# Moving the matmul operands of a fused encoder layer to other places modulo 256 bytes

## The chip, the cores and the metric

The kernel runs on one core of one Trainium2 chip. The metric is the device time of one execution in microseconds; the number that counts is the median of several executions. A profile of one execution gives what each engine did; a matmul runs on the TensorE (PE in the profile), which loads a stationary operand (PEld, the weight load) and streams a moving operand past it. Both are read from the on-chip memory SBUF, 128 partitions of 224 KiB each; the sums go to the eight PSUM banks. VectorE is DVE, ScalarE is ACT, GpSimd is POOL, SyncE is SP.

## The reference

One layer on 512 tokens with a model width of 1024, all float32. Shifts, scales and gates (`sh`, `sc`, `g`) come from a conditioning vector.

```python
h = modulate(rmsnorm(x, norm_ffn1), sh1, sc1)
x = x + 0.5 * g1 * swiglu(h, w_ffn1_in, w_ffn1_out)          # width 2816

h = modulate(rmsnorm(x, norm_mix), sh2, sc2)
qa, ka, va, qb, kb, vb, ga, gb = split(h @ w_in)
ya = window_gqa_sink(rope(norm(qa)), rope(norm(ka)), va, sink) @ w_branch_a
ob = diff_attention(rope(norm(qb)), rope(norm(kb)), vb, lam)
yb = (rmsnorm(ob, subln) * 0.8) @ w_branch_b
x = x + g2 * ((sigmoid(ga) * ya + sigmoid(gb) * yb) @ w_out)

h = modulate(rmsnorm(x, norm_ffn2), sh3, sc3)
x = x + 0.5 * g3 * swiglu(h, w_ffn2_in, w_ffn2_out)
```

## The kernel before

**Arithmetic.** Every float32 operand of a product is split into a high part (rounded to the PE's one-pass float32 type) and the low rest. A product is three matmuls into one bank: high by high, high by low, low by high (`mm3`, L172 to L175; the same three in `two`, L456 to L458). Weights are split by `split_from` (L189): ACT writes the high part, DVE the low one. In the mixer `load_main` (L1115) has ACT write a copy and its negative, and a DMA of POOL's queue adds the weights to the latter.

**Stages in order of time.** The first part of the first feed-forward runs at 512 columns (`first_products`, L703, and `mm3`). From about 82 us it runs in 256 columns: a `Unit` (L460) computes a pair of hidden blocks with seven products of half size instead of eight, named `a11`, `a12`, `s1`, `s2`, `s3`, `s4`, `a22`, each of 4 x 2 x 3 = 24 matmuls. Four times a stretch of 512 columns stands between them: `Out1` (L891), the second matrix of the feed-forward, in four chunks (`CHUNKS`). The last four blocks of the last chunk run by halves, 256 columns (`by_halves`, L906). Three gates follow, also by halves (`first_gates`, L1147), and then the mixer: projections at 512 columns with the weights moving and `h` stationary (`project`), the same in 256 columns (`project_pairs`, L1198), gates at 512 columns (`gates`, L1227), and between them, interleaved by a planner, the scores and products of two attentions (`diff_out` L1403, `window_out` L1640, 256 columns). Then come the branches (`branch`, L1665), the output product (L1729, its last two blocks by halves) and the second feed-forward. That one starts with a plain unit (`Plain`, L1820: four weight sets, no sums) interleaved with `units[1]`, called `lead`, and goes on in units of seven products to the end; the second matrix is also done in units there. The order of the matmuls is the order in which the program lists them.

**Operands of a unit.** The moving operands are the halves of `h` and four sums and differences of them (`SUMS`, L581): `n1`, `n2`, `t3`, `t4`. All lie in the twelve buffers called `b8`, but `n1`, which lies in two of the six buffers called `u4` (L605; `u` in the profile). In the second feed-forward's second matrix a few of the activations lie in `u4` too (L1789). Weights lie in `high` and `low`, two tiles of five places each, which `high_low` (L196) hands out in turn; `aside` shifts a place by so many elements of 4 bytes. Two weight sets of `lead` lie in `b8` (`apart`, L1843), and the weights of the three first gates in `u4` (`spare`, L1144).

**Where the tiles lie.** The allocator puts the groups of equal tiles one behind the other in the order of their first use, each rounded up to 32 bytes per partition. Adding up the sizes gives each start; modulo 256 bytes they are: `x`, `high`, `low`, `ka` and `b8` at 64, `u4` at 160, `raw` and `f2` at 192. All buffers of one group have the same place modulo 256, since their sizes are multiples of 256, and so have all slices that a 256- or 512-column matmul takes from them. In `high` and `low` place i begins at i x 1024 elements plus 64 for each of the first two, both multiples of 256 bytes, plus `aside`. So a weight set lies at 64 with `aside` 0 or `FAR` (64 elements are 256 bytes), at 128 with `ASIDE` (16), at 160 with `TURN` (24). This document calls the stationary operand's place minus that of the moving one, modulo 256 bytes, the **distance** of a matmul.

```python
        i = i * 1024 + min(i, 2) * GAP + aside          # L203, in high_low
        return tuple(t[:, i : i + n] for t in parts)
```

The distances before are then, by stage:

| matmuls | columns | moving | stationary | distance |
|---|---|---|---|---|
| first part, `Out1`, `project`, most gates and branches | 512 | 64 | 64 | 0 |
| units, moving operand in `b8` or `ka` | 256 | 64 | 128 | 64 |
| units, moving operand in `u4` (`n1` and some activations) | 256 | 160 | 128 | 224 |
| last blocks of `Out1`, of a branch, of the output product; `a11`, `a21` of `Plain` | 256 | 64 | 128 or 160 | 64 or 96 |
| three first gates | 256 | 64 | 160 | 96 |
| `project_pairs` | 256 | 128 | 64 | 192 |
| `diff_out`, `window_out`, `s1` of `lead` | 256 | 160 | 64 | 160 |
| `a12` of `lead` | 256 | 64 | 64 | 0 |
| the gate with number `EARLY_A` | 512 | 64 | 128 | 64 |

Of the kernel before, what the change touches and what calls it, by code (L numbers as in the profile page):

```python
# [12 lines left out]
F32R = mybir.dt.float32r  # L13
I32 = mybir.dt.int32
# [4 lines left out]
P = 128  # L19
D = 1024  # L20
T = 512
NC = D // P
NT = T // P
# [9 lines left out]
SH1, SC1, G1, SH2, SC2, G2, SH3, SC3, G3 = range(9)  # L33
# [63 lines left out]

RAW, HILO, F2 = 5, 5, 8

ASIDE, TURN, GAP = 16, 24, 64  # L100

FAR = 64


BRANCH_ASIDES = (ASIDE, TURN, ASIDE, ASIDE), (ASIDE,) * 4
MIX_ASIDES = 0, 0, 0, 0, 0, 0, ASIDE, ASIDE

CHUNKS = (range(0, 6), range(6, 12), range(12, 16), range(16, 22))
PLAIN, LAST_1 = 3, 4
# [24 lines left out]
def layer(ctx: ExitStack, tc: tile.TileContext, a: dict):  # L134
# [13 lines left out]
    def xt():  # L148
        return sbuf("x", [P, T], F32, 8)
# [16 lines left out]
    def keep(shape, nm, dt=F32):  # L166
        return sb.tile(shape, dt, name=nm, tag=nm, bufs=1)
# [28 lines left out]
    def high_low(n=1024, aside=0, holder=None):  # L196
        while turn[0] % HILO in holders:
            turn[0] += 1
        i = turn[0] % HILO
        turn[0] += 1  # L200
        if holder:
            holders[i] = holder
        i = i * 1024 + min(i, 2) * GAP + aside  # L203
        return tuple(t[:, i : i + n] for t in parts)

    def let_go(holder):
# [24 lines left out]
    sub8, lam_s, nlam = (keep([P, n], nm) for nm, n in (("sub8", 1), ("lam_s", 2), ("nlam", 1)))  # L231
    rqa, ccol = keep([P, NT, 8], "rqa"), small(NC)
    x = [xt() for _ in range(NC)]
    parts, modv = [], []
    for nm, n in (("high", 6), ("low", 0)):
        parts.append(keep([P, HILO * 1024 + 2 * GAP + ASIDE], nm, F32R))
        modv += [keep([P, NC], f"mod{v}") for v in range(n)]

    def load_by(t, src, n):
# [9 lines left out]
        return w  # L249


    begin, begins, norms = keep([P, 6 * NC], "begin"), {}, {SC1: NORM1, SC2: NORM2, SC3: NORM3}

    def mod_begin(v):
        if v in (SH1, SH2, SH3):
# [204 lines left out]
    class Unit:  # L460
# [12 lines left out]
        MAKE = {"s1": 5, "a11": 3, "a12": 2, "s2": 4, "s4": 2, "s3": 2, "a22": 3}  # L473
        asked, length = ("s1", "a11", "a12", "a22"), 1.0

        in_order = turned = by_columns = ()
        spare, roomy, apart, more = ("s1",), (), (), {"s1": ("s2", "a11"), "s2": ("s4", "a12"), "a11": ("s3", "a21")}

        def place(self, q):
# [14 lines left out]
        def prepare(self, q):  # L494

            if q in self.ready:
                return
            self.ask(q)
            n = self.depth * 2 * P
            if q in self.apart:  # L500
                both = b8().rearrange("p a b -> p (a b)")
                hi, lo = both[:, 0:n], both[:, 1024 : 1024 + n]
            else:
                hi, lo = high_low(n, TURN if q in self.turned else ASIDE, (self, q))
            t = self.at[q]
            with tc.issue_after(copied[0]) if q in self.in_order and copied else nullcontext():
                split_from(hi, lo, t)
            self.ready[q] = hi, lo
            if q in self.more:
                s, src = self.more[q]  # L510
                G.dma_start(t, self.srcs[src], accum_op=ALU.add)
                self.at[s] = t
# [103 lines left out]
    cact = [sbuf("ka", [P, D], F32, 1)]  # L616
    hh, hl = new_h()
    modv += [keep([P, NC], f"mod{v}") for v in range(len(modv), 9)]
    nc.scalar.dma_start(ccol, a["c"])
    tc.keep_in_program_order(nc.scalar.dma_start(par, a["par"]))  # L620
    for c in range(NC):
# [2 lines left out]
    with tc.manual_schedule(engines=BOUND | {mybir.EngineType.SP, mybir.EngineType.Pool}):  # L624
# [24 lines left out]
        def first_loads(k):  # L649
            n = 1 if k else 2  # L650
            scale = mod_load(SC1, k, n=n)
            if k == 0:
                kept.append(keep([P, NT], "pos", I32))
            shift = mod_load(SH1, k, n=n) if k == 0 else None
            raw = sbuf("raw", [P, 1024], F32, RAW)
            load_by(raw, a["w1s"][k], n)
            w1[k] = [scale, shift or mod_load(SH1, k), raw]
# [227 lines left out]
    def in_unit1(p):  # L885
        srcs = {q: a["w1u"][p - PLAIN, i] for i, q in enumerate(("a11", "a12", "a21", "a22"))}
        u = Unit(srcs, 4, h1_operand, in_post1, p % 2)
        u.p, u.in_order = p, ('s2', 's4')
        return u

    class Out1:  # L891
# [17 lines left out]
        def prepare(self, m):  # L909
            if m not in self.ready:  # L910
                self.ask(m)
                aside = FAR if not self.by_halves(m) else TURN if m < NC - LAST_1 + 2 else ASIDE
                if self.final and m == 0:
                    while turn[0] % HILO != 1:
                        turn[0] += 1
                t = self.ready[m] = high_low(self.depth * P, aside, (self, m))
                with tc.issue_after(copied[0]):
                    split_from(*t, self.at[m])
# [279 lines left out]
    def project_pairs(srcs, then):  # L1198

        n = 2 * P  # L1200
        out = [bank("acc") for _ in range(2)]
        for u, src in enumerate(srcs):
            wh, wl = load_main(src, ASIDE)
            for t in range(NT):
                ht = slice(t * P, (t + 1) * P)
                po = out[t // 2][:, t % 2 * n : (t % 2 + 1) * n]
                for i in range(4):
                    k = 4 * u + i
                    w = slice(i * n, (i + 1) * n)
                    first, last = k == 0 and t % 2 == 0, k == NC - 1 and t % 2 == 1  # L1210
                    PE.matmul(po, hh[k][:, ht], wh[:, w], start=first, stop=False, skip_group_check=True)
                    PE.matmul(po, hh[k][:, ht], wl[:, w], start=False, stop=False, skip_group_check=True)
                    PE.matmul(po, hl[k][:, ht], wh[:, w], start=False, stop=last, skip_group_check=True)
                    yield MM3 / 2
        then(out)
# [11 lines left out]
    def gates(more=lambda: True):  # L1227
        while gate_next[0] < 16 and more():
            j = gate_next[0]
            gate_next[0] += 1  # L1230

            wh, wl = load_main(a["w_gate"][j], ASIDE * (j == EARLY_A))
            out = bank("acc")
            for k in range(NC):
                o = k * P
                mm3(out, wh[:, o : o + P], wl[:, o : o + P], hh[k], hl[k], k == 0, k == NC - 1)
                yield MM3
            gate_end(j, out)
# [423 lines left out]
            turns["w"] = (b, g * nk + kc + 1)  # L1662


    def branch(w, j0, o_h, o_l, then, load, r=FULL[0], asides=(0, 0, 0, 0)):  # L1665
        for u in range(4):
            with tc.issue_after(banded_last[0]):
                wh, wl = load(w[u], aside=asides[u])
            for i in range(2):
                j = 2 * u + i  # L1670
                g = f2()[:, r]
                nc.sync.dma_start(g, gate_scr[j0 + j][:, r])
                y = bank("acc")[:, r]
                for k in range(4):
                    o = k * 256 + i * P
                    mm3(y, wh[:, o : o + P], wl[:, o : o + P], o_h[:, k, r], o_l[:, k, r], k == 0, k == 3)
                    yield MM3 * (r.stop - r.start) / T
                then(j, g, y, r)

    def main():  # L1680
        yield from beside(project(vb_w, T, values_b), LATER)
        yield from beside(project(a["w_kb"], T, keys_b), LATER)
        yield from beside(project(a["w_qb"], T, queries_b), LATER)
        yield from beside(gates(lambda: gate_next[0] < EARLY_A), 1)
        while later or asked:
            column(later)
        tables_a()
        yield from project_pairs([a["w_kva"][u] for u in range(2)], keys_a)
        for g in range(2):
            yield from project_pairs([a["w_qa"][2 * g + u] for u in range(2)], lambda ps, g=g: queries_a(ps, g))  # L1690
        yield from gates(lambda: done["b"] < NT)
        line.drain(lambda: done["b"] == NT)
        start_a()
        yield from gates()
        ma = [b8(F32) for _ in range(2)]

        def then_a(j, g, y, r):
            V.scalar_tensor_tensor(ma[j // 4][:, j % 4, r], g, 1.0, y, ALU.add, ALU.mult)
            line.helped(0.6)

        yield from branch(a["w_yb"], 8, ob_h, ob_l, then_a, load_main)
        mix.extend(new_h())
        mh, ml = mix

        def then_b(j, g, y, r):
            V.scalar_tensor_tensor(g, g, 1.0, y, ALU.add, ALU.mult)
            m = ma[j // 4][:, j % 4, r]
            V.tensor_tensor(m, m, g, ALU.add)
            split_from(mh[j][:, r], ml[j][:, r], m)
            line.helped(1.0)  # L1710

        for i, r in enumerate(HALVES):
            line.drain(lambda: done["a"] >= 2 * i + 2)
            yield from branch(a["w_ya"], 0, *wa["o"], then_b, load_halves, r, BRANCH_ASIDES[i])

    mix = []
    line.run(main())
# [120 lines left out]
            V.scalar_tensor_tensor(g, g, -1.0, self.bank[1, t], ALU.mult, ALU.mult)  # L1838

    plain = units[0] = Plain(units[0].srcs, 4, h_operand, None, 0)  # L1840
    plain.turned = ("a11", "a21")
    lead = units[1]
    lead.spare, lead.roomy, lead.apart = ("s1", "a11", "a12"), ("a22",), ("s1", "a12")  # L1843
    for u in units[1:]:
# [254 lines left out]
```

## Time and profile before

| | us |
|---|---|
| median of 3 executions | 1039.54 |
| lowest and highest of them | 1039.32, 1040.16 |
| the profiled execution | 1039.97 |
| its span, first to last instruction | 1038.2 |
| outside its span | 1.77 |

The profiled execution is 0.43 us over the median. Its granted TensorE clock is 1.00 throughout. A row of a group in the profile reads: line, engine, operation, output and inputs by the program's names with buffer numbers left out, shape, count, then busy us, mean ns of one record, and the idle time before. A matmul's record is longer than the distance between two starts, since matmuls are pipelined; the page says that their ends are modelled. Stretches of the trace are named by their time from the span's start.

### The profile page before, as it was taken

The numbers are of one execution on the slowest core, as the hardware profiler recorded it, in microseconds if no ns is written. First come the engines' busy times: TensorE is split into PE (matmuls) and PEld (weight loads), VectorE is DVE, ScalarE is ACT, GpSimd is POOL, SyncE is SP. The second block draws the span as 40 slices with busy tenths as digits, with TensorE's granted clock in tenths as the row PEclk, the third lists the DMA queues.
The fourth block names the chain that finished last, engine by engine and source line by source line (L and its number), as shares of the span: only waits on it lengthen the run. The fifth ranks groups of instructions, "written<-read, shape, count | busy, mean of one in ns | idle before, by whom it ended". The sixth has DMA issues, their size and how long they took to land.

```text
span 1038.2 us, 18851 instructions
## 1 busy us (share of the span) xinstructions
PE 1030.8 (99%) x7346; PEld 951.1 (92%) x7346; DVE 786.9 (76%) x1456; ACT 583.9 (56%) x1014; POOL 162.5 (16%) x190
## 2 busy tenths in 40 slices
PE   9999999999999999999999999999999999999998
PEld 7789899899999998899888888989999999999998
DVE  7786667567796679859782598976899777877877
ACT  6665335244364343667785856525867546654553
POOL 1101110110110100543333101001112112112210
PEclk9999999999999999999999999999999999999999
DMA  9977787966884459796737944974498998989974
GB/s 360 356 238 203 233 231 209 257 166 205 253 203 133 152 192 410 236 288 139 186 69 190 254 134 151 364 252 104 94 237 191 243 229 207 224 223 214 211 156 112
DMA packets 70377, 220.92 MB, mean 213 GB/s; under 512 B 8464, under 2 KB 13200, under 8 KB 70288
## 3 DMA queue, kind: packets, MB, share of 16 engines
q1 hardware_dynamic: 47808, 146.52, 39.0%
q0 software_dynamic: 19344, 68.70, 35.9%
q10 hardware_dynamic: 3136, 4.51, 1.2%
q8 instruction: 57, 0.93, 0.3%
q14 instruction: 32, 0.26, 0.1%
HBM read 209.46 MB, written 10.23 MB: 212 GB/s over the span
## 4 chain that ended last, share of the span: by engine, by line
PE 94%; DMA 2%; DVE 2%; ACT 2%; issue 0%; SPq 0%; DVEq 0%; ACTq 0%
PE acc L457 7%; PE acc L458 7%; PE acc L456 7%; PE sc L457 6%; PE sc L458 6%; PE sc L456 6%; PE sc L173 5%; PE sc L174 5%; PE sc L175 5%; PE acc L173 5%; PE acc L175 5%; PE acc L174 5%; PE tp L1270 2%; DMA raw<-w1s 2%; PE acc L1192 2%; PE acc L1194 2%
## 5 line engine op out<-in xcount | busy, mean ns | idle before, releaser
L189 ACT CAST high<-raw 128x1024 fp32r<-128x1024 f32 (+2 forms) x176 | 158.2, 913 | 152.9 <-PE sc L174 40.4
L189 DVE TENSOR_TENSOR low<-raw,high 128x1024 fp32r<-128x1024 f32 (+2 forms) x176 | 183.2, 1050 | 42.1 <-ACT high L189 40.8
L456 PE MATMUL acc<-b,high 128*128 128x256 f32 x508 | 140.9, 277 | 0.0
L457 PE MATMUL acc<-b,high 128*128 128x256 f32 x508 | 140.7, 277 | 0.1
L458 PE MATMUL acc<-b,low 128*128 128x256 f32 x508 | 140.6, 277 | 0.0
L457 PE MATMUL sc<-b,high 128*128 128x256 f32 x500 | 138.2, 276 | 0.0
L456 PE MATMUL sc<-b,high 128*128 128x256 f32 x500 | 138.1, 276 | 0.0
L458 PE MATMUL sc<-b,low 128*128 128x256 f32 x500 | 138.1, 276 | 0.0
L189 ACT CAST high<-u 128x1024 fp32r<-128x1024 f32 (+1 forms) x73 | 75.5, 1035 | 50.5 <-PE sc L174 20.2
L189 DVE TENSOR_TENSOR low<-u,high 128x1024 fp32r<-128x1024 f32 (+1 forms) x73 | 87.6, 1200 | 20.4 <-ACT high L189 18.8
L173 PE MATMUL sc<-b,high 128*128 128x512 f32 (+1 forms) x272 | 97.5, 358 | 0.0
L174 PE MATMUL sc<-b,high 128*128 128x512 f32 (+1 forms) x272 | 97.2, 357 | 0.0
L175 PE MATMUL sc<-b,low 128*128 128x512 f32 (+1 forms) x272 | 97.1, 357 | 0.0
L457 PEld LDWEIGHTS acc<-b,high 128*128 128x128 f32 x508 | 95.5, 188 | 0.4 <-DVE b L1883 0.3
L456 PEld LDWEIGHTS acc<-b,high 128*128 128x128 f32 x508 | 95.5, 188 | 0.3 <-ACT f L534 0.2
L458 PEld LDWEIGHTS acc<-b,low 128*128 128x128 f32 x508 | 95.4, 188 | 0.0
L458 PEld LDWEIGHTS sc<-b,low 128*128 128x128 f32 x500 | 93.9, 188 | 0.0
L456 PEld LDWEIGHTS sc<-b,high 128*128 128x128 f32 x500 | 93.9, 188 | 0.0
L457 PEld LDWEIGHTS sc<-b,high 128*128 128x128 f32 x500 | 93.9, 188 | 0.0
L173 PE MATMUL acc<-b,high 128*128 128x512 f32 (+1 forms) x240 | 89.0, 371 | 0.0
L175 PE MATMUL acc<-b,low 128*128 128x512 f32 (+1 forms) x240 | 86.7, 361 | 0.0
L174 PE MATMUL acc<-b,high 128*128 128x512 f32 (+1 forms) x240 | 86.5, 361 | 0.0
(397 smaller groups left out, 2715.9 us busy)
## 6 DMA issues: line engine op xcount, KB each, us to landing
u<-w_mod SPq DMA_DIRECT2D x38, 512.0 KB, 8.3
b<-w_mod SPq DMA_DIRECT2D x32, 512.0 KB, 5.5
raw<-w2i SPq DMA_DIRECT2D x31, 512.0 KB, 5.4
u<-w2i POOLq DMA_DIRECT2D x31, 512.0 KB, 6.7
raw<-w1u SPq DMA_DIRECT2D x24, 512.0 KB, 7.1
u<-w1u POOLq DMA_DIRECT2D x24, 512.0 KB, 7.1
raw<-w1o SPq DMA_DIRECT2D x24, 384.0 KB, 4.4
raw<-w_gate SPq DMA_DIRECT2D x16, 512.0 KB, 5.2
```

The lines of the kernel that those rows point to most:

```text
L173: PE.matmul(out, wh, xh, start=first, stop=False)
L174: PE.matmul(out, wh, xl, start=False, stop=False)
L175: PE.matmul(out, wl, xh, start=False, stop=last)
L189: last = S.copy(hi, src), V.tensor_tensor(lo, src, f(hi), ALU.subtract)
L456: PE.matmul(out, wh[:, s], xh, start=first and j == 0, stop=False, skip_group_check=True)
L457: PE.matmul(out, wh[:, s], xl, start=False, stop=False, skip_group_check=True)
L458: PE.matmul(out, wl[:, s], xh, start=False, stop=last and j == 1, skip_group_check=True)
L1192: PE.matmul(out[t][:, 0:n], hh[k][:, ht], wh[:, o : o + n], start=k == 0, stop=False)
L1194: PE.matmul(out[t][:, 0:n], hl[k][:, ht], wh[:, o : o + n], start=False, stop=k == NC - 1)
L1270: PE.transpose(tp[:, j * P : (j + 1) * P], src, ident)
```

## The change

Nothing is computed otherwise, no operation is added or left out, and no order written in the program is changed. What changes are starts in SBUF. A place in `high` and `low` is now 1088 elements long (4352 bytes, a multiple of 256) and has a lead of 16 elements, two pads of 192 and 160 bytes and longer `begin` and `pos` tiles shift what lies behind, and the ring of descriptors for DMAs of POOL's queue is halved to make room.

```diff
-ASIDE, TURN, GAP = 16, 24, 64
+ASIDE, FIRST, GAP = 16, -8, 64
...
-BRANCH_ASIDES = (ASIDE, TURN, ASIDE, ASIDE), (ASIDE,) * 4
-MIX_ASIDES = 0, 0, 0, 0, 0, 0, ASIDE, ASIDE
+MIX_ASIDES = 0, 0, 0, 0, 0, 0, FIRST, ASIDE
...
-        i = i * 1024 + min(i, 2) * GAP + aside
+        i = i * (1024 + GAP) + ASIDE + aside
...
     x = [xt() for _ in range(NC)]
+    keep([P, 48], "pad1")
...
-        parts.append(keep([P, HILO * 1024 + 2 * GAP + ASIDE], nm, F32R))
+        parts.append(keep([P, HILO * (1024 + GAP) + ASIDE], nm, F32R))
...
-    begin, begins, norms = keep([P, 6 * NC], "begin"), ...
+    begin, begins, norms = keep([P, 6 * NC + ASIDE], "begin"), ...
...
-                hi, lo = high_low(n, TURN if q in self.turned else ASIDE, (self, q))
+                hi, lo = high_low(n, self.asides.get(q, ASIDE), (self, q))
...
     modv += [keep([P, NC], f"mod{v}") for v in range(len(modv), 9)]
+    keep([P, 40], "pad2")
...
-                kept.append(keep([P, NT], "pos", I32))
+                kept.append(keep([P, 2 * NC], "pos", I32)[:, 0:NT])
...
         u.p, u.in_order = p, ('s2', 's4')
+        if p == PLAIN:
+            u.asides = {"s1": FIRST}
+        elif 2 * p in [c.start for c in CHUNKS[1:]] or p == PLAIN + 1:
+            u.asides = {"s2": FIRST}
...
-                aside = FAR if not self.by_halves(m) else TURN if m < NC - LAST_1 + 2 else ASIDE
+                aside = (FIRST if m == NC - LAST_1 else ASIDE) if self.by_halves(m) else FAR
...
-            wh, wl = load_main(src, ASIDE)
+            wh, wl = load_main(src, -ASIDE)
...
-            wh, wl = load_main(a["w_gate"][j], ASIDE * (j == EARLY_A))
+            wh, wl = load_main(a["w_gate"][j])
...
-            yield from branch(a["w_ya"], 0, *wa["o"], then_b, load_halves, r, BRANCH_ASIDES[i])
+            yield from branch(a["w_ya"], 0, *wa["o"], then_b, load_halves, r, (ASIDE if i else FIRST,) + (ASIDE,) * 3)
...
-    plain.turned = ("a11", "a21")
+    plain.asides = {"a11": FIRST}
...
-    nc = bacc.Bacc("TRN2", target_bir_lowering=False, num_devices=1, dynamic_dma_scratch_size=4096)
+    nc = bacc.Bacc("TRN2", target_bir_lowering=False, num_devices=1, dynamic_dma_scratch_size=2048)
```

Adding up the sizes again: the first pad puts `high` at 0 modulo 256 instead of 64; `high` is 21824 bytes long, and with the six small tiles behind it `low` is at 0 too. With the new lead of 64 bytes a weight set lies at 64 with `aside` 0 or `FAR`, at 128 with `ASIDE`, at 32 with `FIRST`, at 0 with `-ASIDE`. `b8` and `ka` stay at 64, `u4` moves from 160 to 64, `raw` and `f2` from 192 to 128. So the distances become:

| matmuls | distance before | after |
|---|---|---|
| 512 columns | 0 (one gate: 64) | 0 |
| units, moving operand in `b8` or `ka` | 64 | 64 |
| units, moving operand in `u4` | 224 | 64 |
| the first weight set behind a stretch of 512 columns (`s1` of the first unit; `s2` of units 4, 6, 8; block 4 of the last `Out1`; set 0 of the first half branch; block 6 of the output product) | 224, 64, 96, 64, 64 | 224 |
| other blocks by halves there | 64 or 96 | 64 |
| `a11` of `Plain`, `a21` of `Plain` | 96, 96 | 224, 64 |
| three first gates | 96 | 0 |
| `project_pairs` | 192 | 64 |
| `diff_out`, `window_out`, `s1` of `lead` | 160 | 0 |
| `a12` of `lead` | 0 | 0 |

More of the change, by code (lines that the diff above doesn't have):

```diff
@@ L249, in mod_load @@
         return w
-    begin, begins, norms = keep([P, 6 * NC], "begin"), {}, {SC1: NORM1, SC2: NORM2, SC3: NORM3}
+    begin, begins, norms = keep([P, 6 * NC + ASIDE], "begin"), {}, {SC1: NORM1, SC2: NORM2, SC3: NORM3}
     def mod_begin(v):
@@ L474, in layer @@
         asked, length = ("s1", "a11", "a12", "a22"), 1.0
-        in_order = turned = by_columns = ()
+        in_order, by_columns, asides = (), (), {}
         spare, roomy, apart, more = ("s1",), (), (), {"s1": ("s2", "a11"), "s2": ("s4", "a12"), "a11": ("s3", "a21")}
@@ L1662, in window_out, with branch @@
             turns["w"] = (b, g * nk + kc + 1)
-    def branch(w, j0, o_h, o_l, then, load, r=FULL[0], asides=(0, 0, 0, 0)):
+    def branch(w, j0, o_h, o_l, then, load, r=FULL[0], asides=(0,) * 4):
         for u in range(4):
```

## The prediction

> **What bounds the kernel.** I read the page first: the busy shares and the chain of waits.
>
> ```profile
> span 1038.2 us, 18851 instructions
> PE 1030.8 (99%) x7346; PEld 951.1 (92%) x7346; DVE 786.9 (76%) x1456; ACT 583.9 (56%) x1014; POOL 162.5 (16%) x190
> PE 94%; DMA 2%; DVE 2%; ACT 2%; issue 0%; SPq 0%; DVEq 0%; ACTq 0%
> ```
>
> PE is 94% of the chain that ends last, and no other engine is above 76%. So the pace of the matmuls themselves sets the time, and I asked for the groups of PE with shapes kept apart.
>
> ```profile
> L174 PE MATMUL sc<-b,high 128*128 128x512 f32 x192 | 74.8, 390 | 0.0
> L456 PE MATMUL acc<-b,high 128*128 128x256 f32 x508 | 140.9, 277 | 0.0
> L457 PE MATMUL acc<-u,high 128*128 128x256 f32 x80 | 22.3, 279 | 0.0
> L457 PE MATMUL sc<-u,high 128*128 128x256 f32 x72 | 20.1, 280 | 0.0
> L1212 PE MATMUL acc<-low,b 128*128 128x256 f32 x96 | 26.9, 280 | 0.0
> L175 PE MATMUL op<-u,b 128*128 128x256 f32 x72 | 20.3, 282 | 0.0
> L456 PE MATMUL acc<-b,b 128*128 128x256 f32 x8 | 2.3, 283 | 0.0
> ```
>
> The last column is idle time: there is none. Yet a matmul of 256 columns takes 277 to 283 ns, and what differs between the rows is where the operands lie: distance 64 in the second row, 224 in the third and fourth, 192, 160 and 0 in the last three. To turn a record into a pace, I took three neighbouring stretches, of 24, 24 and 144 matmuls by the timeline, from the view of stretches, and the records within the first and the last.
>
> ```profile
> 142.57:145.40 2.83, 2.83 (x26) 1.00 0.91 262
> 145.40:148.20 2.80, 2.80 (x26) 1.00 1.02 399
> 148.20:164.50 16.30, 16.30 (x146) 1.00 1.00 263
> L457 PE MATMUL acc<-b,high 128*128 128x256 f32 x8 | 2.2, 281 | 0.0
> L457 PE MATMUL acc<-b,high 128*128 128x256 f32 x24 | 6.6, 276 | 0.0
> ```
>
> The first stretch needs 2.83 / 24 = 117.9 ns per matmul with a record of 281, the third 16.30 / 144 = 113.2 with 276. So a nanosecond of record is about one of pace, and the records can be used as prices. But both stretches have distance 64, on the same operand groups. The distance alone does not decide: at 64 there is a **light** pace (276) and a **heavy** one (281). Heavy is what follows a stretch of 512 columns; the 24 matmuls at 224 in between (`n1`) turn it light. Other stretches, each a row of a window of its own, in order of time:
>
> ```profile
> L457 PE MATMUL acc<-b,high 128*128 128x256 f32 x21 | 5.9, 281 | 0.0
> ...
> L174 PE MATMUL sc<-b,high 128*128 128x256 f32 x11 | 3.1, 280 | 0.0
> ...
> L174 PE MATMUL sc<-b,high 128*128 128x256 f32 x12 | 3.4, 281 | 0.0
> ...
> L174 PE MATMUL acc<-b,u 128*128 128x256 f32 x36 | 10.1, 280 | 0.0
> ...
> L174 PE MATMUL acc<-b,high 128*128 128x512 f32 x7 | 2.8, 395 | 0.0
> ...
> L174 PE MATMUL acc<-b,high 128*128 128x256 f32 x8 | 2.2, 280 | 0.0
> ...
> L174 PE MATMUL sc<-b,high 128*128 128x256 f32 x18 | 5.1, 281 | 0.0
> ```
>
> They are: behind a wait of PE at 315 us (64, heavy); the last blocks of the first feed-forward at 340 us (distance 96) and 344 us (64, heavy); the three first gates at 364 us (96); the one gate of 512 columns at distance 64, at 502 us; a branch set at 649 us (96); the output product at 701 us (64, heavy, right behind 512 columns).
>
> **The change, part by part.** Nothing issued changes, so each part is a count of matmuls times a difference of records. (a) Moving operands in `u4`: the lines L456 to L458 have 3 x (80 + 72) = 456 of them at 279 to 280. 24 stay at 224 (the first set at 82 us); 432 go to distance 64. If they run light, 432 x 3.5 ns = -1.5 us. (b) The three sets `s2` behind `Out1`: 72 matmuls from 281 to the 280 of distance 224, -0.1. (c) End of the first feed-forward: from 340 us on 36 matmuls at 280, 36 at 281, later 18 more at 280; with the first block at 224 the rest should be light: 18 x 4 + 36 x 5 + 18 x 4 ns, -0.3. (d) The three first gates go from 96 to 0, 144 matmuls. The nearest row for 0 at 256 columns is 283 (`acc<-b,b`): about +0.35, since a part of them is slow already. (e) The gate of 512 columns goes from 64 to 0, 395 to 389 or 390: 24 x 6 ns, -0.15. (f) Half branch: 24 from 281 to 280, 24 from 280 to 276, -0.1. (g) Output product: 24 from 281 to 276, 24 from 281 to 280, and 15 of the second half from light to 280, -0.1. (h) `Plain`: half of its 96 matmuls at 96 go to 64, -0.15. (i) `diff_out`, `window_out` and `s1` of `lead`, 216 + 24 at 160, go to 0: from 282 to 283, +0.2. (k) `project_pairs`, 288 matmuls, from 192 to 64: its 280 is no lighter than the heavy 281 of distance 64. It starts right behind 512 columns and is cut by transposes and scores throughout, so I take heavy again: 0. (l) Behind each of some 20 stretches at 224 the first matmuls are still slow. The sequence shows it at one return:
>
> ```profile
> L456 PE MATMUL acc<-b,high 128*128 128x256 f32 x1 | 0.3, 284 | 0.0
> ```
>
> Two or three such of 5 to 8 ns per return go with (a): -0.3.
>
> The sum is -1.5 - 0.1 - 0.3 + 0.35 - 0.15 - 0.1 - 0.1 - 0.15 + 0.2 - 0.3 = **-2.15 us**. The profiled execution took 1039.97; the median is 0.43 lower, and the difference applies to it alike: 1039.54 - 2.15 = 1037.4 us.
>
> Costs the trace does not show, from both sides. Distance 0 at 256 columns was seen in few places, always near 283; the other bound is the light 276, as 512 columns at 0 show their lowest record. That would make (d) -0.6 and (i) -1.5 instead of +0.35 and +0.2; I keep 283, the row with the same columns. (k) is bounded by 276, -1.3 us, and by 283, +0.8. The new 224 has the stationary operand half a 64-byte step off where the old one had the moving operand off; that is a rival below. The other engines also read and write the moved tiles:
>
> ```profile
> L189 DVE TENSOR_TENSOR low<-raw,high 128x1024 fp32r<-128x1024 f32 x104 | 126.4, 1221 | 29.3 <-ACT high L189 28.1
> L189 DVE TENSOR_TENSOR low<-u,high 128x1024 fp32r<-128x1024 f32 x67 | 81.9, 1222 | 19.8 <-ACT high L189 18.3
> x<-x_scr POOLq DMA_DIRECT2D x8, 256.0 KB, 6.0
> L1723 POOL DMA_DIRECT2D x<-x_scr x8: 543/558/582, 636.5 to 646.6; - x8
> ```
>
> `raw` at 192 and `u` at 160 cost DVE the same 1221 and 1222 ns, so I cost their moves at nothing. The halved ring could hold up POOL's issues where many stand together; the densest group is these eight loads of `x`, 6.0 us each, issued from 636.5 to 646.6 us and first used behind the first block of the output product, which begins at 668 us: some 20 us of cover against 6 us, nothing. Places now never overlap, which removes possible waits of ACT and DVE for PE; PE's idle column is 0.0, so nothing again.
>
> A rule speaks against all of this. The Trainium skill, in "SBUF — State Buffer", section "SBUF: two separate sides", says that on the engine side only the port pair shared by VectorE and GpSimd causes contention and that "PE, ACT, and DVE's dedicated pair never wait on anyone"; by it the sum is 0 and the time 1039.5. The rows above do not agree: 276 against 281 and 283 ns with no idle time before, at the same granted clock.
>
> **The rivals.** (1) *The tail gets heavy: slower.* From 746 us to the end all is at 64, but for `n1` and its like at 224 every 18 us or so. Once these are at 64 too, nothing is left that turns a heavy pace light. Right before, at 743 us, stand the 24 matmuls of `s1` of `lead`, from now on at distance 0.
>
> ```profile
> 746.30:1038.20 291.90, 288.25 (x2534) 288.05 (x2532) 232.92 (x354) 169.01 (x256) 51.07 (x59) 1.00 0.87 204
> 315.72 0.38 PE L456 MATMUL acc<-b,high 128*128 128x256 f32 x1
> 315.94 0.28 PE L457 MATMUL acc<-b,high 128*128 128x256 f32 x1
> ```
>
> If they leave it heavy, or one wait of PE does, as the late matmul at 315.72 us did for all 78 that follow it (281, above), 2534 x 4.6 ns = +11.7 us come on top of the rest, less the -1.1 of (a) and (l) that lies there: 1037.4 + 11.7 + 1.1 = 1050. It decides at the first matmuls behind 746 us. For it: in 512 columns distance 0 is followed by heavy. Against it: the tail has no wait of PE before, and every stretch at another distance that was entered light was left light:
>
> ```profile
> L457 PE MATMUL acc<-b,high 128*128 128x256 f32 x4 | 1.1, 283 | 0.0
> ...
> L456 PE MATMUL tp<-u,b 128*128 128x256 f32 x8 | 2.3, 282 | 0.0
> L457 PE MATMUL op<-b,high 128*128 128x256 f32 x8 | 2.2, 276 | 0.0
> ```
>
> The first is distance 96 at 721 us with light matmuls before and behind; the second `s1` of `lead` at 160, and the third what follows it. (2) *The new 224 does not turn the pace.* Then the four unit stretches between the `Out1` stretches, some 1100 matmuls behind their first sets, run at 281, not 276 for most: about +4.3 us, and the 0.75 of (a) to (c) that lies there is lost: 1037.4 + 5.0 = 1042.4. For it: with the stationary operand half a step off (distance 96), 340 us was followed by heavy. Against: all stretches at 224 so far were followed by light. (3) *More is gained:* `project_pairs` runs light, -1.3, or the stretches at 0 behind 512 columns do: 1036.1 or less, down to 1034.8. (4) *The change does not do what it says*: the pace hangs on something else that goes with the tile, and (a) does not come: within 1 us of 1039.5. For it: all stretches at 224 so far also had `u4` as the moving tile, so the trace cannot part tile from distance there. Against: 281 and 276 were seen on the same tiles. The rule of the Trainium skill above stands beside this rival.
>
> **How the numbers follow.** Chances: forecast 0.62, with its own range 1036.4 to 1038.6, of which 0.34 lies beyond 0.2% and 0.28 within; tail heavy 0.14; new 224 fails 0.08; more gained 0.10; nothing 0.06. 0.2% is 2.1 us, about what a measurement of this kernel can tell from no change. So faster is 0.34 + 0.10 = 0.44, same 0.28 + 0.06 = 0.34, slower 0.14 + 0.08 = 0.22. The range 1034.8 to 1042.5 takes in all but the heavy tail and some hundredths at the lower end.
>
> **What would show it.** In the profile after, the rows `acc<-u,high` and `sc<-u,high` at L457 fall to 276 if (a) is right; if they read 280 or 281, (a) is wrong. The stretch from 746 us on: 276 in all rows, or 281 for rival 1. The units behind each `Out1` read 280 for 24 matmuls, then 276; 281 there is rival 2. `acc<-b,u` rises to 283 and `op<-u,b` stays near 282 if distance 0 is heavy. `acc<-low,b` at L1212 stays at 280; 276 is rival 3. New idle time before PE in any stretch would make the whole sum wrong, since it knows no waits.

## The result and the profile after

| | before | after |
|---|---|---|
| median of 5 executions, us | 1039.45 | 1048.38 |
| lowest and highest, us | 1039.13, 1040.16 | 1047.78, 1050.30 |
| the profiled execution, us | 1039.97 | 1047.78 |
| its span, us | 1038.2 | 1046.0 |

The changed kernel is slower by 0.9%: the ratio is 1.0088, with a 95% interval from 1.0073 to 1.0103. The forecast was 1037.4 us; the time lies above the range, near the 1050 us of rival 1, which had a chance of 0.14.

These are rows of the changed kernel's page: the span, the busy time of the engines, the shares of the chain of waits, and two of the largest groups of matmuls.

```profile
span 1046.0 us, 18850 instructions
...
PE 1039.3 (99%) x7346; PEld 960.3 (92%) x7346; DVE 788.3 (75%) x1456; ACT 583.6 (56%) x1014; POOL 163.1 (16%) x190
...
PE 95%; DMA 2%; DVE 1%; ACT 1%; issue 0%; SPq 0%; DVEq 0%; ACTq 0%
...
L456 PE MATMUL acc<-b,high 128*128 128x256 f32 x508 | 142.5, 281 | 0.0
...
L457 PE MATMUL sc<-b,high 128*128 128x256 f32 x500 | 139.9, 280 | 0.0
```

The same 7346 matmuls keep PE busy 8.5 us longer (1030.8 before), and the other engines do what they did. PE is 95% of the chain and its idle column is still 0.0. Nothing waits more; the matmuls themselves are slower. The group `acc<-b,high` at L456 had a mean record of 277 ns and now has 281.

Where the time lies shows in the view of stretches. This is the second feed-forward of the changed kernel, behind `s1` of `lead`, to the end (columns: window, its length, then busy time and instruction count of PE, PEld, DVE, ACT and POOL, granted clock, DMA share, GB/s).

```profile
744.00:1046.00 302.00, 298.34 (x2534) 298.14 (x2532) 233.62 (x354) 168.74 (x256) 51.20 (x59) 1.00 0.85 197
```

The row for the same 2534 matmuls before, from 746.30 us on, stands in the prediction: 291.90 us. So this part lost 302.0 - 291.9 = 10.1 us, at the same granted clock. All that lies ahead of it gained 746.3 - 744.0 = 2.3 us. Together that is the +7.8 us of the span.

The groups of PE in single windows of the changed kernel, in order of time (the fourth and fifth rows are of the whole span):

```profile
L456 PE MATMUL acc<-u,high 128*128 128x256 f32 x8 | 2.2, 276 | 0.0
...
L457 PE MATMUL acc<-b,high 128*128 128x256 f32 x8 | 2.2, 280 | 0.0
...
L174 PE MATMUL sc<-b,low 128*128 128x256 f32 x19 | 5.3, 281 | 0.0
...
L174 PE MATMUL acc<-b,u 128*128 128x256 f32 x48 | 13.6, 283 | 0.0
...
L1217 PE MATMUL acc<-low,b 128*128 128x256 f32 x96 | 26.7, 278 | 0.0
...
L457 PE MATMUL tp<-u,b 128*128 128x256 f32 x8 | 2.3, 284 | 0.0
...
L457 PE MATMUL acc<-b,high 128*128 128x256 f32 x316 | 88.9, 281 | 0.0
```

They are: `n1` in a unit at 145 to 180 us, now at distance 64 and light; a first set at the new 224, at 213 us; the halves at the end of the first feed-forward behind the block at 224, at 341 us, heavy; the three first gates at distance 0; `project_pairs`; `s1` of `lead` at distance 0, at 741 us; and the tail from 744 us to the end, heavy throughout. The last row holds the 10 us.

### The profile page after: what moved, and what is told of

The parts are those of the page before. It is cut to its first block, busy times and chain, and to the rows that moved or that the text cites. A ratio compares the mean times of both kernels' runs of the same rounds, so it can differ in the third digit from the quotient of the medians.

```text
span 1046.0 us, 18850 instructions
## 1 busy us (share of the span) xinstructions
PE 1039.3 (99%) x7346; PEld 960.3 (92%) x7346; DVE 788.3 (75%) x1456; ACT 583.6 (56%) x1014; POOL 163.1 (16%) x190
## 4 chain that ended last, share of the span: by engine, by line
PE 95%; DMA 2%; DVE 1%; ACT 1%; issue 0%; SPq 0%; DVEq 0%; ACTq 0%
PE acc L457 7%; PE acc L456 7%; PE acc L458 7%; PE sc L457 6%; PE sc L456 6%; PE sc L458 6%; PE sc L172 5%; PE sc L174 5%; PE sc L173 5%; PE acc L172 5%; PE acc L174 5%; PE acc L173 5%; PE tp L1275 2%; PE sc L185 2%; DMA raw<-w1s 2%; PE acc L1198 2%
## 5 line engine op out<-in xcount | busy, mean ns | idle before, releaser
L456 PE MATMUL acc<-b,high 128*128 128x256 f32 x508 | 142.5, 281 | 0.0
L457 PE MATMUL acc<-b,high 128*128 128x256 f32 x508 | 142.3, 280 | 0.1
L457 PE MATMUL sc<-b,high 128*128 128x256 f32 x500 | 139.9, 280 | 0.0
L456 PE MATMUL sc<-b,high 128*128 128x256 f32 x500 | 139.9, 280 | 0.0
L456 PEld LDWEIGHTS acc<-b,high 128*128 128x128 f32 x508 | 96.9, 191 | 0.3 <-ACT f L534 0.2
L456 PEld LDWEIGHTS sc<-b,high 128*128 128x128 f32 x500 | 95.3, 191 | 0.0
```

The source lines that it names most:

```text
L456: PE.matmul(out, wh[:, s], xh, start=first and j == 0, stop=False, skip_group_check=True)
L457: PE.matmul(out, wh[:, s], xl, start=False, stop=False, skip_group_check=True)
```

## The experiments

In all of them the base is the changed kernel, and light and heavy mean what they mean in the prediction: a record of 276 or of 281 ns at distance 64, a pace of 113.3 or 117.8 ns. Two questions were open. Is the tail slow only because it is entered heavy, with nothing left to turn it? And what makes it heavy at the entry: is the heavy pace carried in from `Plain` through `s1` of `lead` (A), or does a set at distance 0 leave heavy whatever came before (B)?

### One turn ahead of the tail

The first set behind `lead` goes to distance 224.

```diff
+    units[2].asides = {"a11": FIRST}
```

> The changed kernel, with one weight set more at distance 224: the 24 matmuls of a11 of the first unit behind s1 of lead, at 744 us. Theory A (the pace at distance 64 is carried on from what came before, and s1 of lead at distance 0 was entered heavy and left heavy) and theory B (24 matmuls at distance 0 always leave the heavy pace, however they were entered) both say: the set at 224 turns the pace, all 2508 matmuls behind it have records of 276 ns, not 281, and the time is 1048.4 - 11.2 = 1037.2 us. Rival C (the tail is slow since its moving operands in u4 now lie at 64, or for another reason of its tiles, not by the pace carried in): the records stay at 281 and the time at 1048.

The median of 10 executions is 1037.76 us, against 1040.15 for the kernel before on the same chip; the ratio is 1.0002, 0.9971 to 1.0034, unclear. The reason for the wide interval is in the single times: six lie from 1037.12 to 1038.02, one at 1039.32, and three at 1047.31, 1047.33 and 1049.81. The profiled one is one of the three, so it shows what spoiled the tail there; the other two have no trace. Groups of PE from 747.1 to 765.9 us and from 766.2 us on:

```profile
L457 PE MATMUL sc<-b,high 128*128 128x256 f32 x24 | 6.6, 276 | 0.0
...
L457 PE MATMUL sc<-b,high 128*128 128x256 f32 x276 | 77.6, 281 | 0.0
```

The 24 matmuls at 224 did turn the pace light, with the same tiles in the same places, so rival C of the expectation falls; 19 us later the pace went heavy for all the rest. The timeline at that point (start, duration, engine, line, operation), first PE, then ACT:

```profile
765.97 0.28 PE L458 MATMUL sc<-b,low 128*128 128x256 f32 x1
766.08 0.33 PE L456 MATMUL acc<-b,high 128*128 128x256 f32 x1
766.25 0.28 PE L457 MATMUL acc<-b,high 128*128 128x256 f32 x1
...
765.39 0.59 ACT L534 COPY f<-acc 128x512 f32<-128x512 f32 x1 [0.58 <-DVE f L1767]
```

The starts are 110 to 120 ns apart, then once 170 ns, at the first matmul of a new bank; ACT copied a bank `acc` out until 765.39 + 0.59 = 765.98 us. That this copy held it is inferred from the times here; in the last experiment the profile names it as the releaser at such a place. Behind a hold of some 60 ns on PE, too short for the idle column, the tail took about 10 us more. So a turn ahead of the tail brings it down to the forecast, but in three of ten executions a single one did not hold.

### `u4` back at its old place

The second pad goes, so that `u4` lies at 160 again, and with it `n1` at distance 224 in every unit; the rest of the change stays.

```diff
-    keep([P, 40], "pad2")
```

> The changed kernel without its second pad, so that u4 lies at 160 again: n1 and some activations are back at distance 224, the first gates at 96, diff_out, window_out and s1 of lead at 160; all else as changed. Theories A and B: the tail can enter heavy behind s1 of lead, but the first n1 some 72 matmuls later turns it light, so records of 276 from there on. Gains (b), (c), (e) to (h) stay, -1.0 at most, 0.3 to 0.5 us are lost at the head of the tail, (a), (d) and (i) are undone: 1038.6 to 1039.2 us. Rival C: light as well, so it does not tell C from A and B; what it tells is whether moving u4 alone brought the 11 us.

Measured: 1039.47 us (10 executions), ratio to before 0.9989, 0.9979 to 0.9998. Groups of PE in three windows, 745.6 to 753.8, 754.1 to 756.7 and 756.9 us to the end:

```profile
L457 PE MATMUL acc<-b,high 128*128 128x256 f32 x8 | 2.2, 281 | 0.0
...
L457 PE MATMUL acc<-u,high 128*128 128x256 f32 x8 | 2.2, 280 | 0.0
...
L457 PE MATMUL acc<-b,high 128*128 128x256 f32 x308 | 85.0, 276 | 0.0
```

`s1` of `lead`, at distance 160 here, is entered heavy and leaves heavy; 72 matmuls later the first `n1` at 224 turns the pace, and the tail is light to the end. So 8.9 of the 11 us that separate the changed kernel from its forecast hang on this one pad (some 10 by the two ratios to the kernel before, 1.0088 and 0.9989): the sets at 224 that cost 3.5 ns per matmul were also what kept the tail light.

### Entering `s1` of `lead` light

Both extra sets of `Plain` go to 224, so that the pace is light ahead of `s1` of `lead` at distance 0.

```diff
-    plain.asides = {"a11": FIRST}
+    plain.asides = {"a11": FIRST, "a21": FIRST}
```

> The changed kernel with a21 of Plain at 224 too, so that its second half begins with 48 matmuls at 224 in a row instead of 6 and 6 in turn with distance 64. The 48 matmuls at 64 that follow should be light (276) where the changed kernel has 281 from 734.7 us on, so that s1 of lead at distance 0 is entered light. Theory A: the tail then stays light, about 1037.3 us. Theory B: distance 0 leaves it heavy all the same, about 1048.2 us.

Measured: 1048.69 us, one execution. Groups of PE from 736.6 to 741.8 us, ahead of `s1` of `lead`, and from 745 us on, behind it:

```profile
L457 PE MATMUL sc<-b,high 128*128 128x256 f32 x16 | 4.4, 276 | 0.0
...
L457 PE MATMUL acc<-b,high 128*128 128x256 f32 x316 | 88.8, 281 | 0.0
```

48 light matmuls, then 24 at distance 0, then 2532 heavy ones without a wait of PE between them. A falls: in this execution the set at distance 0 left heavy although it was entered light.

### Single sets at other distances, in a light tail

The tail gets one turn, and then single sets of 24 at other distances, with turns between them. With the moving operand at 64, an `aside` of 0 gives distance 0, `24` gives 96, `-ASIDE` gives 192 and `40` gives 160.

```diff
+    units[2].asides = {"a11": FIRST}
+    for p, at in ((4, 0), (5, FIRST), (6, 24), (7, FIRST), (8, -ASIDE), (9, FIRST), (10, 40)):
+        units[p].asides = {"a11": at}
```

> As e1, so that the tail begins light, with probes in it: a11 (24 matmuls) of unit 4 at distance 0, of unit 6 at 96, of unit 8 at 192, of unit 10 at 160, and each time a11 of the next unit at 224 to set the pace back. Theory A: the matmuls at 64 behind the probe at 0 stay at 276 and the time is about 1037.5 us. Theory B: the 480 matmuls behind the probe at 0 have 281, +2.1 us, until the next 224; about 1039.5. Of 96, 192 and 160 no theory is stated: before, 160 left light what came light, 96 too; 192 was not seen from light.

Measured: 1040.11 us, one execution. Groups of PE ahead of the set at distance 0, in it, and behind it (747.1 to 796.3, 796.5 to 799.15, 799.3 to 855.7 us):

```profile
L457 PE MATMUL sc<-b,high 128*128 128x256 f32 x64 | 17.7, 276 | 0.0
...
L457 PE MATMUL acc<-b,high 128*128 128x256 f32 x8 | 2.3, 283 | 0.0
...
L457 PE MATMUL acc<-b,high 128*128 128x256 f32 x72 | 20.2, 281 | 0.0
```

432 light matmuls, 24 at distance 0, 480 heavy ones up to the next turn; those cost 480 x 4.5 ns = 2.2 us. The sets at 96, 192 and 160 were entered light and left light. So of the distances tried only 0 spoils a light pace, and B holds. A wait of PE, 0.40 us between two starts, did not spoil the pace here:

```profile
765.92 0.28 PE L458 MATMUL sc<-b,low 128*128 128x256 f32 x1
766.32 0.39 PE L456 MATMUL acc<-b,high 128*128 128x256 f32 x1
766.54 0.28 PE L457 MATMUL acc<-b,high 128*128 128x256 f32 x1
```

### The same in a heavy tail

Here the tail is left heavy at its start, and single sets are tried as turns (`32` gives distance 128, `8` gives 32).

```diff
+    for p, at in ((3, 0), (4, 24), (5, 40), (6, -ASIDE), (7, 32), (8, 8), (9, FIRST)):
+        units[p].asides = {"a11": at}
```

> The changed kernel, whose tail begins heavy, with probes of 24 matmuls in it: a11 of unit 3 at distance 0, unit 4 at 96, unit 5 at 160, unit 6 at 192, unit 7 at 128, unit 8 at 32, unit 9 at 224. From the runs so far: 0 leaves heavy what is heavy (281 behind it), 224 turns it light (276 for the last 540 matmuls). If the pace is carried on by all other distances, as 96, 160 and 192 carried on the light one, all matmuls at 64 before unit 9 have 281 and the time is 1048.4 - 2.4 = 1046.0 us. If 96 alone turns it as well (24 matmuls of it did at 649 us before the change), it is about 1038.6 plus what a later probe spoils.

Measured: 1040.92 us, one execution. Groups of PE ahead of the set at distance 96 and behind it (782.6 to 799.4 and 802.4 to 855.9 us):

```profile
L457 PE MATMUL sc<-b,high 128*128 128x256 f32 x32 | 9.0, 281 | 0.0
...
L457 PE MATMUL acc<-b,high 128*128 128x256 f32 x72 | 19.9, 276 | 0.0
```

24 matmuls at 96 turn the pace as 24 at 224 do. That was one of the two outcomes, with 1038.6 us for it; the time is 2.3 us above. Some 1930 matmuls at 64 behind the turn are light, which takes 1930 x 4.5 ns = 8.7 us off the 1047.78 us of the changed kernel's profiled execution and gives 1039.1, half a microsecond over the figure expected. The rest is the clock: granted at 0.50 from 28.24 to 31.65 us in this execution. The first matmul of 256 columns starts at 83.72 us here and at 82.03 in the changed kernel, 1.7 us later in a part where the two kernels are alike. The sets at 160, 192, 128, 32 and 224 that follow were all entered light and left light, so this run does not tell whether 192, 128 or 32 turns a heavy pace (160 did not, in the second experiment).

### Several turns in the tail

Five units of the tail begin with a set at 224, so that a spoilt pace is turned back soon.

```diff
+    for p in (2, 3, 5, 7, 9):
+        units[p].asides = {"a11": FIRST}
```

> The changed kernel with a11 of units 2, 3, 5, 7 and 9 at distance 224: e1 with four turns more along the tail. Theory B with waits (distance 0 leaves heavy, a set of 24 at 224 makes light, a wait of PE at 766 us makes it heavy again in some executions and only a next turn ends that): all executions between 1037.3 and 1038.5 us, none near 1047, as a spoilt stretch now ends after at most 650 matmuls, and usually at unit 3, 10 us behind the wait. Each turn costs 24 x 3.4 ns = 0.08 us, 0.4 in all against the low executions of e1 (1037.2): median 1037.6. Rival: the high executions of e1 are slow for another reason (the chip, its clock); then some stay near 1047 here as well.

Measured: 1037.60 us, median of 10 executions from 1036.91 to 1039.11; the kernel before has 1039.72 on the same chip, and the ratio is 0.9977, 0.9968 to 0.9987. No execution is near 1047. The profiled one, its page and a group of PE from 744.2 us on:

```profile
span 1035.1 us, 18850 instructions
...
L457 PE MATMUL acc<-b,high 128*128 128x256 f32 x316 | 87.2, 276 | 0.0
```

This is the changed kernel with five sets of the tail at another distance, and it is faster than the changed kernel and than the one before. It is 2.1 us under the latter, where the forecast had -2.15 us. That the two agree so closely is partly luck: the five turns cost 0.4 us that the forecast did not have, and the trace of the changed kernel has gains ahead of the tail that it did not reckon with (the next section).

### 36 matmuls at 224 in place of 18

The last experiment adds to this one a second block at 224 at the end of the first feed-forward, where 18 matmuls at 224 had left a heavy pace.

```diff
-                aside = (FIRST if m == NC - LAST_1 else ASIDE) if self.by_halves(m) else FAR
+                aside = (FIRST if m < NC - LAST_1 + 2 else ASIDE) if self.by_halves(m) else FAR
...
+    for p in (2, 3, 5, 7, 9):
+        units[p].asides = {"a11": FIRST}
```

> e6 with the first two of the last four blocks of the last Out1 at 224, 36 matmuls instead of 18. In the changed kernel 18 of them left the 54 behind them heavy, while 24 always made light, and the records at 224 come in a cycle of four (113, 116, 118, 120 ns apart). If the number counts by that cycle, 36 leave light: 36 matmuls behind them at 276 instead of 281, 18 at 280 instead of 281, in all 0.2 us less than e6, too little to see in the time but plain in the records. If not, they stay at 281.

Measured: 1038.17 us (1037.08 to 1040.34, 10 executions), ratio 0.9981, 0.9972 to 0.9991: faster than before, and not to be told from the experiment without the second block. The groups of PE from 342.95 to 346.9 us, behind the two blocks, and from 821.3 to 855.3 us, and the timeline between:

```profile
L173 PE MATMUL sc<-b,high 128*128 128x256 f32 x12 | 3.3, 276 | 0.0
...
L457 PE MATMUL sc<-b,high 128*128 128x256 f32 x40 | 11.2, 281 | 0.0
```

```profile
820.88 0.28 PE L458 MATMUL op<-b,low 128*128 128x256 f32 x1
821.34 0.39 PE L456 MATMUL acc<-b,high 128*128 128x256 f32 x1 [0.19 <-ACT f L534]
821.57 0.28 PE L457 MATMUL acc<-b,high 128*128 128x256 f32 x1
```

After 36 the pace is light, where 18 had not done it. What was won there (36 x 4.5 ns, under 0.2 us) was lost in the profiled execution to a wait at 820.88 us: ACT's copy came late, the pace went heavy, and stayed so until the next turn at 855 us, some 1.8 us (290 x 4.5 ns and some 0.5 us of the wait itself). The turn then bounded the loss, as meant. An earlier wait in the same execution, 0.53 us from the start at 765.85 us to the next one, left the pace light.

## Why the prediction was wrong

**The bound** was read rightly: the pace of the matmuls sets the time, no wait of PE was added, and both paces at distance 64 are there after as before.

**The step that failed** is in rival 1, where the forecast was chosen against it: "every stretch at another distance that was entered light was left light". The two stretches quoted for it lie at distances 96 and 160. The changed kernel puts `s1` of `lead` at 0, and no stretch of 256 columns at 0 that was entered light stood in the trace of before. The prediction carried the observation over to it. The third and fourth experiments show that 0 is the exception: 24 matmuls at 0, entered light, left 2532 and 480 heavy ones behind them. Besides, the entry was not light in the changed kernel at all: `Plain`'s 54 matmuls ahead of `s1` of `lead` ran heavy. The rest of rival 1 came as written: with `n1` at 64, nothing turned the pace back. Its price was 2534 x 4.6 ns = 11.7 us for a heavy tail against a light one; the trace gives 302.0 us after against 290.9 us for the sixth experiment's tail (744.2 to 1035.1 us), 11.1 us.

**(a), (b) and (l)** were right where the tail is not concerned: the units of the first feed-forward are light behind every first set, `n1` included. Comparing the starts of the same matmuls in both traces, they gained 0.8 us between 82 and 312 us, against the 0.8 that the terms hold there (1.5 + 0.1 + 0.3 less the 1.1 in the tail). A wait at 314 us left the pace light where the one at 315 us before had left it heavy, another 0.3 us, on which nothing was reckoned:

```profile
314.21 0.28 PE L458 MATMUL acc<-b,low 128*128 128x256 f32 x1
314.48 0.39 PE L456 MATMUL acc<-b,high 128*128 128x256 f32 x1
314.70 0.28 PE L457 MATMUL acc<-b,high 128*128 128x256 f32 x1
```

The same matmul starts 0.27 us behind the one ahead of it in all nine profiled executions of this document, and each time the pace ahead of it is light. Behind it the pace was heavy in three of them (the kernel before, the second and the third experiment) and light in six. So these 0.3 us are chance, in the kernel before too. (Up to the next 512 columns 65 matmuls follow it, not the 78 of the prediction.) In the tail (a) has the wrong sign in effect: the prediction priced `n1` by its own 3.5 ns a matmul and took what the set does for those behind it as a rival.

**(c)** came to nothing in place of -0.3: the 18 matmuls at 224 did not turn the pace, and 54 heavy ones followed. The trace of before had only turns of 24. **(h)** came to +0.1 to +0.2 in place of -0.15 for the same reason: in `Plain` the sets at 224 come six matmuls at a time, and what follows is heavy.

**(d)** was mis-sized: the three first gates went from 280 to 283 ns, but the first of them were slow before too (120 ns a matmul), and the starts of the 144 give +0.15 against +0.35. **(e), (f) and (g)** came within 0.05 us of -0.15, -0.1 and -0.1. **(i)** was taken as +0.2 and is 0: the part of the mixer with nearly all of them took the same time in both traces, with mean records of 283 in the two later products of each three where distance 160 had 281 and 282. Here the forecast priced the set itself nearly right and missed what it leaves behind.

**(k)** was taken as 0 and gained 0.7 us: `project_pairs` starts heavy behind 512 columns, but most of its stretches behind transposes run light, and the mean record goes from 280 to 278. That is a part of rival 3, inside its bound of -1.3.

**Rival 2** is refuted: the new 224 has the same 280 and is followed by light in all five places with 24 matmuls behind 512 columns or at a branch (`s2` of three units, the half branch, the output product). **Rival 4** does not fit the runs: one pad of 160 bytes is worth some 9 us, and five sets of 24 matmuls at another place 1.1% (ratios to the kernel before of 1.0088 and 0.9977). Which tile the operands are in decides nothing: `n1` in `u4` at 64 is light. The rule of the Trainium skill beside it ("SBUF — State Buffer", section "SBUF: two separate sides") says that PE never waits on anyone there. It speaks of waits between engines, and whether PE waits on another engine at SBUF no run here shows. What the runs show is a pace that changes with the places of PE's own two operands, 119.9 ns at distance 0 against 113.3 at 64; so the 1039.5 us that the prediction drew from the rule does not follow from it.

Of the 2.3 us gained ahead of the tail 0.5 lies before 82 us, where no distance of a matmul changes. All of it is there at the 69th matmul, which starts at 14.60 us before and at 14.09 after; in the nine profiled executions that start lies anywhere from 13.60 to 14.61 us, so this gain is within their scatter.

## What to carry to other kernels

Where an engine is never idle and the same instruction has two durations, ask not only what each place costs but which state each stretch leaves behind: an edit that removes a costly instruction may remove what restored the cheap state for hundreds of others. An observation of the form "every stretch so far" covers the values it was seen at; a new value in a place from which a long stretch inherits its state is to be priced by the whole stretch. If a state can be lost to a chance wait, a cheap turn repeated is safer than one turn ahead: with five of them in 290 us the highest execution was 1039.11 us, with one three of ten were above 1047.

## What the runs showed of the hardware

- The pace of 256-column matmuls at distance 64 is one of two, 113.3 or 117.8 ns, and either one was seen to last: 2532 matmuls heavy in the changed kernel, nearly all of the tail light in the second experiment with sets at 224 between, and 648 light without any between two turns of the sixth.
- What a set of 24 costs by itself, in ns per matmul: distance 0 119.9, 160 119.6, 32 and 128 118.2, 224 116.5; 96 took 117.2 from heavy and 120.1 from light; 192 took 113.3 from light. Sets of 24 at 224 and at 96 turned heavy to light, 36 at 224 did too, 18 and 6 did not. Nor did 36 at 96 at 340 us of the kernel before, which 281 follows at 344 us (both rows are in the prediction); so the count alone does not decide, and why these did not is open. Distance 0 is the only one seen to turn light to heavy.
- A wait of PE turns light to heavy at times: a hold of some 60 ns did (766.08 us, first experiment), and one of 0.46 us between two starts at 820.88 us in the last; waits of 0.40 us at 765.92 us in the fourth and of 0.53 us at 765.85 us in the last did not. One of 0.27 us at the same matmul, at 314 to 316 us, did in three of nine executions. So its length does not decide.
- What decides it is open, and so is what the two paces are: the traces show the weight load and the matmul only as whole records, with no sign of what one holds against the other.
